# Layer 0 of a two-layer transformer kernel: the first projection K-tile by K-tile behind its modulation, and a step's transposes ahead of its values

## The chip, the core and the metric

The kernel runs on one core of a Trainium2 chip. A core has TensorE (PE in the profile; its weight loads are PEld), VectorE (DVE), ScalarE (ACT), GpSimd (POOL), and SyncE (SP), whose queue starts nearly all DMA transfers here. The metric is device time in microseconds, the median of several runs; the profile is one execution of the same program.

## The reference, cut to what matters

512 latent tokens of width 1024, and 256 context tokens, pass two layers. Layer 0 has sixteen heads of 64, in four groups: each of four key/value heads serves four query heads. Two groups attend in a window (with a sink), two to all tokens. Everything is float32.

```python
mx = (silu(c) @ mod_w[l] + mod_b[l])            # six parts of 1024: shift, scale, gate, twice
hx = _rms(x, norm_mix_w[l]) * (1.0 + scx1) + shx1     # modulated input; the same for ctx with c_ctx
q, k, v = heads(hx @ w_in)                      # q and k: RMS norm per head, rotary for latent tokens
p = softmax(q @ k.T * scale)                    # window mask and sink in the first two groups
out = (p @ v) @ w_out
x = x + gx1 * out
x = x + gx2 * swiglu(_rms(x, norm_ffn_w[l]) * (1.0 + scx2) + shx2)
```

Layer 1 is a differential attention with the same frame. The change does not touch it.

## The kernel before, in words

Tokens lie in six tiles of 128: 0 to 3 latent, 4 and 5 context; `CTX_FIRST` is the order 4, 5, 0, 1, 2, 3. Products that need full precision are made of three fast ones: an operand is split into a high part (`hi`, rounded by ACT) and a remainder (`lo`, a subtraction), and hi x hi, hi x lo and lo x hi are summed in PSUM. The 1024 inputs are eight K-tiles; a projection of one token tile for one key/value head (384 columns: four queries, key, value) is 24 matmuls.

The kernel is written as one program in a natural order, and a scheduler then sets the order of each engine's instructions by dependencies, buffers and priorities. Each engine keeps its order at run time.

**The start.** `start_mod(n)` makes shift and scale (parts 0 and 1) for quarter n of the width, two K-tiles: mod weights (0.5 MB pieces) come by DMA, matmuls with a 32-wide padded operand give partial rows (`mod`, L171), ACT copies them (`modr`, L174), two small matmuls with a selection matrix add them up as columns (`modcol`, L179), and DVE adds the bias (`modc`, `aff`). In between, each token tile is normed (`nh`, L843 and L844), turned by TensorE (`npt`, L848) and copied to `xT` (L849). Then all of `xT` is modulated K-tile by K-tile (L854) and split into `hT`, or `hTc` for context (L859, L860). Only behind all this are the weights of the first head loaded and split (`weights0`; `wir`, `wih`, `wil`, L309 and L310), and `in_proj0` projects tile after tile (`inps`, L405 to L407), each summed over all eight K-tiles at once.

**A tile of a projection** is copied by ACT (`qkv`), normed per head and rotated (`rotate`: DVE, ACT, and POOL for `rs_q`, `qy`, `kd` and the copy of the values, `vv`), and turned by TensorE (`qpt`, `kpt`) into `qt` and `kT`.

**The attention of layer 0**, `attend0`, is a generator for one step, that is one key/value head and one tile of queries. It makes scores of two query heads (`sc`, L509), maxima on DVE, exponentials on ACT (`Pt`, L523), and scales them on POOL (L533), twice with a `yield` behind each. Then for each pair of key blocks of 128 it turns the probabilities (`ppt`, L543; two PSUM banks, tr0 and tr1), copies them out (`PT`, ACT and DVE by turns, L548 and L546), and sums values (`av`, L553; two halves of the output side by side in the array). Probabilities lie in tiles of one head, six buffers. `Staggered` emits the first scores of a step, then the last step's whole rest, then the second scores. Meanwhile the next head is projected, a tile per step; its `qkv` has two buffers. In the fourth head's loop the output projection (`ops`) starts.

## Time and profile before

| what | us |
|---|---|
| runs, lowest, median, highest | 1823.11, 1824.57, 1825.61 |
| the profiled execution: its own time, its span | 1825.45, 1823.7 |
| TensorE busy in the span | 1752.0 |
| VectorE, ScalarE, GpSimd busy | 1002.0, 825.5, 641.8 |
| start to the first scores of layer 0 | 72.4 |
| layer 0's mixer from there to the first FFN matmul | 72.4 to 447.6 |
| FFN of layer 0 | 447.6 to about 1040 |
| layer 1's mixer, then its FFN | to about 1453, then to the end |

In the lines shown below, a group of instructions has line, engine, operation, tiles written and read, shapes and count; then busy time and the mean in ns of one; then idle time of the engine ahead of them, and what ended it. A row of the timeline has start, duration, engine, line, operation, tiles and count, and in brackets an idle time. A row of waits reads: who waited for whom, us in total, times, longest. A duration on TensorE includes the pipeline; the time from start to start tells what an instruction really takes up.

### The profile page before, as it was taken

To read this page: it belongs to the slowest core of one execution; us is meant where nothing else is said; L and a number is where in the kernel's file an instruction comes from. 1 tells how busy PE (TensorE), PEld (TensorE's weight loads), DVE (VectorE), ACT (ScalarE), POOL (GpSimd) and SP (SyncE) were. 2 spreads that over 40 slices of the span, in tenths; PEclk is the share of its full clock that TensorE was granted. 3 is DMA by queue.
4 is the path that set the end of the run, shared out by engine and by line. 5 is a ranking of instruction groups with operands and counts; after the bars stand their busy time and mean duration, and the time that the engine had idled before them with its cause. 6 is when DMAs were issued, how large, how long until landed. Compare 5 with 4: busy or idle time off the path is not lost. (4 is left out here: it accounts for less than half of the span.)

```text
span 1823.7 us, 26198 instructions
## 1 busy us (share of the span) xinstructions
PE 1752.0 (96%) x9958; PEld 1458.2 (80%) x9958; DVE 1002.0 (55%) x1703; ACT 825.5 (45%) x1726; POOL 641.8 (35%) x840
## 2 busy tenths in 40 slices
PE   6999999999999999999999899999998999999998
PEld 4877676667888888888888789999986888888886
DVE  4664545443355555545552657777675455655652
ACT  6555555544354444333331656666664532222220
POOL 2764554632053443222220466666643200000000
PEclk8999999999999999999999899999999999999999
DMA  9111322302543334334330311111103233232221
GB/s 314 46 44 55 96 73 99 131 13 76 180 149 117 103 104 140 115 127 126 117 105 3 102 35 59 44 45 44 42 25 104 90 97 102 82 104 93 93 93 47
DMA packets 152478, 165.65 MB, mean 91 GB/s; under 512 B 16480, under 2 KB 139936, under 8 KB 152352
## 3 DMA queue, kind: packets, MB, share of 16 engines
q1 hardware_dynamic: 152000, 163.77, 28.1%
q8 instruction: 78, 1.28, 0.3%
q14 instruction: 48, 0.39, 0.1%
q10 hardware_dynamic: 352, 0.21, 0.0%
HBM read 159.73 MB, written 4.22 MB: 90 GB/s over the span
## 5 line engine op out<-in xcount | busy, mean ns | idle before, releaser
L750 PE MATMUL pg<-hT,wgh 128*128 128x512 f32 (+1 forms) x736 | 244.8, 386 | 2.2 <-ACT hT L293 2.2
L750 PE MATMUL pu<-hT,wuh 128*128 128x512 f32 (+1 forms) x736 | 244.1, 385 | 0.0
L412 DVE TENSOR_TENSOR dps<-dps,g 128x512 f32<-128x512 f32 x200 | 135.7, 697 | 131.3 <-PE dps L801 126.7
L799 PE MATMUL dps<-wdh,hdh 128*128 128x512 f32 x440 | 176.2, 401 | 5.3 <-DVE x L413 3.5
L800 PE MATMUL dps<-wdl,hdh 128*128 128x512 f32 x440 | 174.0, 396 | 0.0
L801 PE MATMUL dps<-wdh,hdl 128*128 128x512 f32 x440 | 166.4, 396 | 0.0
L750 PEld LDWEIGHTS pg<-hT,wgh 128*128 128x128 f32 x736 | 137.2, 189 | 32.7 <-ACT hT L293 2.4
L750 PEld LDWEIGHTS pu<-hT,wuh 128*128 128x128 f32 x736 | 137.1, 189 | 28.5
L750 PE MATMUL pg<-hT,wgl 128*128 128x512 f32 (+1 forms) x368 | 141.9, 386 | 0.0
L750 PE MATMUL pu<-hT,wul 128*128 128x512 f32 (+1 forms) x368 | 141.5, 384 | 0.0
L413 DVE TENSOR_TENSOR x<-x,dps 128x512 f32<-128x512 f32 x200 | 133.3, 683 | 3.3
L405 PE MATMUL inps<-wih,hT 128*128 128x384 f32 x384 | 133.1, 347 | 0.4 <-ACT qkv L451 0.2
L406 PE MATMUL inps<-wil,hT 128*128 128x384 f32 x384 | 130.6, 340 | 0.0
L407 PE MATMUL inps<-wih,hT 128*128 128x384 f32 x384 | 130.6, 340 | 0.0
L198 ACT ACTIVATE modw<-modw,cols 128x256 f32<-128x256 f32 x192 | 81.9, 498 | 69.4 <-DMA modw<-in_mod_w_dram 66.4
L799 PEld LDWEIGHTS dps<-wdh,hdh 128*128 128x128 f32 x440 | 82.7, 188 | 27.6 <-DVE x L413 4.4
L310 DVE TENSOR_TENSOR wul<-wur,wuh 128x1024 fp32r<-128x1024 f32 x44 | 54.6, 1241 | 89.3 <-ACT wuh L309 89.3
L801 PEld LDWEIGHTS dps<-wdh,hdl 128*128 128x128 f32 x440 | 82.6, 188 | 20.2 <-issue 0.4
L750 PE MATMUL pg<-hTc,wgh 128*128 128x256 f32 x352 | 98.3, 283 | 0.5 <-ACT hTc L293 0.2
L750 PE MATMUL pu<-hTc,wuh 128*128 128x256 f32 x352 | 98.2, 282 | 0.0
L800 PEld LDWEIGHTS dps<-wdl,hdh 128*128 128x128 f32 x440 | 82.8, 188 | 17.6
L777 DVE TENSOR_TENSOR pu<-sg,pu 128x768 f32<-128x768 f32 (+1 forms) x44 | 36.5, 829 | 108.3 <-PE pu L750 94.4
(235 smaller groups left out, 4306.3 us busy)
## 6 DMA issues: line engine op xcount, KB each, us to landing
modw<-in_mod_w_dram SPq DMA_DIRECT2D x96, 512.0 KB, 4.0
wgr<-in_ffn_w_in_dram SPq DMA_DIRECT2D x44, 512.0 KB, 3.4
wur<-in_ffn_w_in_dram SPq DMA_DIRECT2D x44, 512.0 KB, 3.4
wdr<-in_ffn_w_out_dram SPq DMA_DIRECT2D x44, 512.0 KB, 3.5
wir<-in_od_w_in_dram SPq DMA_DIRECT2D x96, 128.0 KB, 2.3
x<-in_x_dram SPq DMA_DIRECT2D x8, 512.0 KB, 3.9
wir<-in_ev_w_in_dram SPq DMA_DIRECT2D x16, 256.0 KB, 2.7
wor<-in_ev_w_out_dram SPq DMA_DIRECT2D x8, 512.0 KB, 4.4
```

The source lines that it names most:

```text
L198: nc.scalar.activation(pr[:, k], w[:, k], AF.Copy, scale=cols[:, kk:kk + 1])
L310: (sub or nc.vector).tensor_sub(lo, raw, f32(hi))
L405: nc.tensor.matmul(ps, hs[0][:, k, :], a, start=k == 0, stop=False)
L406: nc.tensor.matmul(ps, hs[0][:, k, :], b, start=False, stop=False)
L407: nc.tensor.matmul(ps, hs[1][:, k, :], a, start=False, stop=k == KT - 1)
L412: nc.vector.tensor_mul(tmp, ps, g[:, n * 512:(n + 1) * 512])
L413: eng.tensor_add(xt[:, n * 512:(n + 1) * 512], xt[:, n * 512:(n + 1) * 512], tmp)
L750: nc.tensor.matmul(ps[:, s0:s1], a, cols_T(b, s0, s1)[:, k, :], start=k == 0 and q == 0, stop=k == KT - 1 and q == 2)
L777: nc.vector.tensor_mul(pu, sg, pu)
L799: nc.tensor.matmul(ps, hh, a, start=j == 0, stop=False)
L800: nc.tensor.matmul(ps, hh, b, start=False, stop=False)
L801: nc.tensor.matmul(ps, hl, a, start=False, stop=j == nj - 1)
```

## The change

- **First head, start.** The modulation of parts 0 and 1 is made a quarter at a time (`start_mods`), both parts in one PSUM tile and one `modr`. Behind each quarter `start_h` modulates and splits its two K-tiles (some of the modulation goes from DVE to ACT), and `project` sums only these K-tiles, for six token tiles that stand in six PSUM banks. The head's weights come unit by unit (`unit0`) right behind the mod weights of their quarter, through `raw_tile` with two buffers, and their remainders go from DVE to POOL. Half of the `xT` copies go from ACT to DVE.
- **Modulation columns**, in all chunks: two transposes and a DVE reduce over four partial rows (`mod_cols`) instead of two matmuls with the selection matrix.
- **Attention of layer 0.** Four heads' probabilities lie in one tile `P4`, two buffers. All transposes of a step come first, the turned blocks are written back into `P4`, then a new `yield`, then all values. `Pairs` emits first scores of a step, the last step's transposes, second scores, the last step's values. In the fourth head's loop the output projection of a tile follows half a step later.
- `qkv` has five buffers instead of two, for all heads of layer 0.

```diff
-PBUF0 = 6
+QBUF = 5
@@ mod_chunk
-        pc2 = p_1.tile([P, nb, 2], F32, name="modcol", tag=bank)
+        add_mod(l, part, k0, k1, mod_cols(r, p_1.tile([P, nb, P], F32, name="modcol", tag=bank)), 2)
+
+    def mod_cols(r, ps):
+
+        nb = ps.shape[1]
         for b in range(nb):
-            nc.tensor.matmul(pc2[:, b, :], r[:, b * P:(b + 1) * P], sel2, start=True, stop=True)
-        add_mod(l, part, k0, k1, pc2, 2)
+            nc.tensor.transpose(ps[:, b, :], r[:, b * P:(b + 1) * P], ident)
+        m = small.tile([P, nb, 2], F32, name="mcol", tag=f"mcol{nb}")
+        nc.vector.tensor_reduce(m, ps.rearrange("p b (j r) -> p b r j", r=32)[:, :, 0:2, :], AX.X, ALU.add)
+        return m
@@
-    def project(ps, t, ws, c0, c1):
+    def project(ps, t, ws, c0, c1, ks=range(KT)):
...
-        for k in range(KT):
+        for k in ks:
@@ in_proj0
-            ps = acc_tile("inps", 384, one=0) if b else p_sc.tile([P, 1024], F32, name="inps", tag="sc")[:, :384]
-            project(ps, t, ws, 0, 384)
-            raw = wp.tile([P, 384], F32, name="qkv", tag="qkv", bufs=2)
+            if banks:
+                ps = banks[t]
+            else:
+                ps = acc_tile("inps", 384, one=0)
+                project(ps, t, ws, 0, 384)
+            raw = rp.tile([P, 384], F32, name="qkv", tag="qkv", bufs=QBUF)
@@ attend0
-        Pt = [None] * 4
+        P4 = mp.tile([P, 4, TOK], F32, name="Pt", tag="Pt", bufs=2)
+        Pt = [P4[:, h, :] for h in range(4)]
...
-        for g0 in range(0, nk, 2):
-            PTs = []
-            for kc in range(g0, min(g0 + 2, nk)):
...
-                PT = mp.tile([P, 4, P], F32, name="PT", tag="PT", bufs=4)
-                if kc % 2:
-                    nc.vector.tensor_copy(PT, pt)
-                else:
-                    nc.scalar.copy(PT, pt)
-                PTs.append((kc, PT))
-
-            for kc, PT in PTs:
...
+        for kc in range(nk):
+            pt = tr_tile("ppt", [P, 4, P], one=kc % 2)
+            cs = slice(kc * P, (kc + 1) * P)
+            for h in range(4):
+                nc.tensor.transpose(pt[:, h, :], Pt[h][:, cs], ident)
+
+            if kc % 2:
+                nc.vector.tensor_copy(P4[:, :, cs], pt)
+            else:
+                nc.scalar.copy(P4[:, :, cs], pt)
+        yield
+
+        for kc in range(nk):
+            for j in range(2):
+                nc.tensor.matmul(av[64 * j:64 * j + 64, :], vv[:, vt[kc], :], P4[:, j::2, kc * P:(kc + 1) * P],
+                                 start=kc == 0, stop=kc == nk - 1)
@@
+    class Pairs:
...
+        def push(self, gen):
+
+            self.flush()
+            self.new, self.last = gen, self.new
             next(gen)
+            if self.last:
+                next(self.last)
+
+        def step(self):
+
+            next(self.new)
             self.flush()
@@
+    def start_mods(n):
+
+        ps = tr_tile("mod", [P, 2, 256])
         for part in range(2):
...
+        r = start.pool.tile([P, 512], F32, name="modr", tag="modr", bufs=1)
+        nc.scalar.copy(r, ps.rearrange("p a n -> p (a n)"))
+        m = mod_cols(r, tr_tile("modcol", [P, 4, P]))
+        for part in range(2):
+            add_mod(0, part, 2 * n, 2 * n + 2, m[:, 2 * part:2 * part + 2], 2)
+
+    def start_h(n, segs):
+
+        ks = slice(2 * n, 2 * n + 2)
+        for s0, s1 in segs:
+            i = s0 // SEQ
+            for k in range(2 * n, 2 * n + 2):
+                z = xT[:, k, s0:s1]
+                sc, sh = aff[0][:, 0, k, i:i + 1], modc[0][:, 0, k, i:i + 1]
+                if k % 2:
+                    nc.scalar.activation(z, z, AF.Identity, bias=sh, scale=sc)
+                else:
+                    nc.vector.tensor_scalar(z, z, sc, sh, ALU.mult, ALU.add)
+            hi, lo = (cols_T(j, s0, s1)[:, ks, :] for j in range(2))
+            nc.scalar.copy(hi, xT[:, ks, s0:s1])
+            (nc.gpsimd if i else nc.vector).tensor_sub(lo, xT[:, ks, s0:s1], f32(hi))
@@
-    start_mod(0)
-    start_mod(1)
+    start_mods(0)
+    ws = [unit0(0, 0, wp.pool, nc.gpsimd)]
...
+    banks = {t: acc_tile("inps", 384) for t in CTX_FIRST[:2]}
+    for t in (0, 2):
+        two = p_sc.tile([P, 2, 512], F32, name="inps", tag="sc")
+        banks.update({t + a: two[:, a, :384] for a in range(2)})
+    for n in range(4):
+        if n:
+            start_mods(n)
+            ws.append(unit0(0, n, wp.pool, nc.gpsimd))
+        start_h(n, ((SEQ, TOK), (0, SEQ)) if n else ((SEQ, TOK), (0, SEQ // 2), (SEQ // 2, SEQ)))
+        for t in CTX_FIRST:
+            project(banks[t], t, ws, 0, 384, range(2 * n, 2 * n + 2))
...
-    att = Staggered()
+    att = Pairs()
...
-                if b == 3 and hp == 0 and 0 < t <= 5:
+                if b == 3 and hp == 1 and 0 < t <= 5:
```

83 lines of the change are left out of this document (39 added, 44 removed).

## The prediction

> **What bounds the kernel now.** I read the page's first two parts, then a table of stretches, then TensorE's timeline where its clock or its busy share falls, then waits and groups of the layer-0 mixer. Of the page: the span, TensorE's busy time, its busy share and its granted clock in 40 slices of 45.6 us.
>
> ```profile
> span 1823.7 us, 26198 instructions
> PE   6999999999999999999999899999998999999998
> PEclk8999999999999999999999899999999999999999
> ```
>
> TensorE is busy nearly throughout, so what counts is PE time that does no work. Slice 1 is the only bad one, and the first part of the change sits there. The table of stretches (busy time of each engine, then granted clock, DMA share, GB/s):
>
> ```profile
> 0.00:6.70 6.70, 0.00 (x0) 0.00 (x0) 0.00 (x0) 3.40 (x6) 0.54 (x6) 1.00 0.69 235
> 6.70:20.00 13.30, 11.50 (x74) 6.11 (x74) 3.08 (x8) 7.22 (x14) 2.68 (x6) 1.00 1.07 397
> 20.00:28.00 8.00, 5.29 (x50) 4.06 (x51) 4.38 (x9) 6.67 (x15) 3.66 (x7) 1.00 1.07 374
> 28.00:40.80 12.80, 9.81 (x85) 5.53 (x83) 8.98 (x20) 6.95 (x13) 1.86 (x1) 0.67 1.04 330
> 40.80:46.00 5.20, 5.20 (x19) 5.20 (x20) 5.20 (x11) 3.63 (x7) 3.75 (x1) 0.51 0.27 79
> 46.00:72.40 26.40, 26.01 (x155) 25.14 (x156) 18.76 (x38) 12.38 (x29) 19.21 (x25) 1.00 0.09 21
> 72.40:92.30 19.90, 17.86 (x98) 16.12 (x97) 11.55 (x37) 12.32 (x35) 17.74 (x30) 0.91 0.27 75
> 92.30:310.00 217.70, 212.53 (x1503) 157.32 (x1501) 116.03 (x310) 121.36 (x324) 112.45 (x175) 0.99 0.23 71
> 350.00:447.60 97.60, 91.49 (x461) 67.28 (x461) 38.54 (x71) 41.16 (x84) 30.69 (x33) 1.00 0.10 33
> ```
>
> Until 40.8 the DMA engines are full and TensorE has small work only; from 40.8 to 72.4 the first head's projection runs with the DMA idle. That is the serial pair which the change folds together. The attention (92 to 447) looks full, but a busy PE need not be efficient; the timeline shows where (start, duration, count, and idle time in brackets):
>
> ```profile
> 374.45 1.08 PE L553 MATMUL av<-PT,vv 128*64 128x256 f32 x8
> 375.47 1.09 PE L543 MATMUL ppt<-cst,Pt 128*128 128x128 f32 x8
> 376.80 0.65 PE L553 MATMUL av<-PT,vv 128*64 128x256 f32 x4 [0.24 <-ACT PT L548]
> 377.38 0.66 PE L543 MATMUL ppt<-cst,Pt 128*128 128x128 f32 x4
> 377.97 0.65 PE L553 MATMUL av<-PT,vv 128*64 128x256 f32 x4
> 378.55 0.66 PE L543 MATMUL ppt<-cst,Pt 128*128 128x128 f32 x4
> ```
>
> By starts, one key block of values and one of transposes, alternating, take 378.55 - 377.38 = 1.17 us. Two blocks of each in one alternation take 376.56 - 374.45 = 2.11 us (without the 0.24 of waiting) where two alternations take 2.34. Each alternation costs 0.23 us.
>
> **Part 1: the start.** All K-tiles came after all modulations; now each quarter (two K-tiles, 36 matmuls over six tiles) follows its own modulation. Before and now, the end of the start on TensorE (mod: modulation matmuls; modcol: their turn to columns; inps: projection):
>
> ```order
> L171 MATMUL mod<-modw,s_pad 32x256 x12
> L179 MATMUL modcol<-cst,modr 128x2 x2
> L171 MATMUL mod<-modw,s_pad 32x256 x8
> L179 MATMUL modcol<-cst,modr 128x2 x2
> L405 MATMUL inps<-wih,hTc_112 128x384
> ```
>
> Now, behind the third quarter's projection:
>
> ```order
> L411 MATMUL inps<-wil,hT_110 128x384
> L412 MATMUL inps<-wih,hT_111 128x384
> L868 MATMUL mod<-modw,s_pad 32x256 x2
> L182 MATMUL modcol<-cst,modr 128x128 x4
> L410 MATMUL inps<-wih,hTc_112 128x384
> ```
>
> Only one quarter is left behind the last modcol, but nothing stands between the two on TensorE to cover the modulation's way through ACT and DVE. On ACT, the second quarter's modr copy now stands behind the norms of all six tiles (nh, xT); it was two copies, the first of them ahead of the fifth and sixth tile. Before:
>
> ```order
> L849 COPY xT<-npt 128x4x128
> L843 ACTIVATE nh,nss<-x_201 128x1024
> L174 COPY modr<-mod 128x256
> L849 COPY xT<-npt 128x4x128 x2
> L843 ACTIVATE nh,nss<-x_203 128x1024
> ```
>
> Now the sixth tile's copies come first:
>
> ```order
> L889 CAST hT_110<-xT 128x2x256
> L907 COPY xT<-npt 128x4x128 x2
> L314 CAST wih<-wir 128x768
> L885 ACTIVATE xT<-xT,modc_106,aff_108 128x256
> L889 CAST hT_110<-xT 128x2x256
> L871 COPY modr<-mod 128x512
> ```
>
> The second quarter's modulation moved behind that row.
>
> The rows that price this (timeline and groups):
>
> ```profile
> 28.01 1.07 ACT L849 COPY xT<-npt 128x512 f32<-128x512 f32 x2
> 44.45 0.52 PE L407 MATMUL inps<-wih,hTc 128*128 128x384 f32 x1
> 44.77 0.52 PE L405 MATMUL inps<-wih,hTc 128*128 128x384 f32 x1
> 46.13 0.34 PE L406 MATMUL inps<-wil,hTc 128*128 128x384 f32 x1
> 46.30 0.34 PE L407 MATMUL inps<-wih,hTc 128*128 128x384 f32 x1
> 72.43 0.39 PE L509 MATMUL sc<-kT,qt 128*128 128x256 f32 x2
> 92.35 0.60 PE L543 MATMUL ppt<-cst,Pt 128*128 128x128 f32 x4
> L849 ACT COPY xT<-npt 128x512 f32<-128x512 f32 x12 | 6.6, 590 | 4.8 <-PE npt L848 4.7
> L309 ACT CAST wih<-wir 128x768 fp32r<-128x768 f32 x5 | 4.1, 832 | 0.0
> L860 DVE TENSOR_TENSOR hT<-xT,hT 128x512 fp32r<-128x512 f32 x6 | 5.0, 849 | 0.0
> ```
>
> A projection matmul is issued every 0.17 us (46.13 to 46.30) at full clock, every 0.32 at a granted 0.5 (44.45 to 44.77).
>
> - SP's queue: up to the last mod weight go 13.5 MB (six tiles and 16 pieces of 0.52 MB, four weight units of 0.39, 0.4 of constants). The stretches moved 1.6, 5.3 and 3.0 MB by 28 us; the other 3.6 MB at 374 GB/s land by 38 us. Four weight units now go between; the four tiles of x have four pieces and one unit ahead of them instead of six pieces, and come earlier.
> - Second quarter: the six norms end at 29.1 (28.01 + 1.07), so modulation, cast and first matmul come at about 32. From there 36 x 0.174 = 6.3 us a quarter: 38.5, then 45, and with 1 us of small waits 46. By then the last weights have long landed.
> - Last quarter: modr copy 0.6 (512 wide, as xT), four transposes 0.5, DVE's reduce and adds 0.9 (part 2), modulation 0.6 to 1.0 (256 and 512 wide), a wih cast (0.83) that stands between on ACT, hi cast 0.6: about 5 us in which TensorE stands. Then 6.3 us, 0.6 of waiting for DVE's lo part, and 1.7 because the clock falls after such a gap (0.91 over 19.9 us in the stretch at 72.4 is 1.8 lost): end at about 60.5.
> - Then: before, the first softmax transposes (ppt) stand at 92.35, with 213 inps, 16 sc, 24 qpt and 11 kpt issued; now with 285, 8, 24 and 12, since the second head's projection fills TensorE while six tiles are rotated. From 60.5: 141 x 0.174 = 24.5, 36 transposes of q and k at the 0.12 of a ppt 4.3, scores 1, and about 3.5 of waiting for the first rotated tile on POOL. That is 93.8. Before, 72 more projections (12.5) less eight scores (0.9) would be done at 103.9. **Gain 10.1.**
>
> POOL takes the first head's weight remainders from DVE, and the second head's stand ahead of the rotations there:
>
> ```profile
> L149 POOL TENSOR_TENSOR rs_q<-rs_q,neghalf 128x5 f32<-128x5 f32 x24 | 28.5, 1188 | 1.2
> L310 POOL TENSOR_TENSOR wil<-wir,wih 128x768 fp32r<-128x768 f32 x11 | 20.1, 1829 | 3.7 <-ACT wih L309 3.6
> L454 POOL TENSOR_TENSOR qy<-qy,rs_q 128x320 f32<-128x320 f32 x24 | 17.3, 722 | 0.9
> L461 POOL TENSOR_TENSOR kd<-qy,kd 128x128 fp32r<-128x128 f32 x24 | 11.7, 488 | 10.6 <-ACT kd L460 5.1 <-ACT es L527 2.1 <-PE sc L509 1.6
> ```
>
> By the order, up to the first kd POOL does three rs_q (3.6), one wil, one qy and small copies: 10 us from 60.5, against 8.4 us of projections on TensorE. Hence the wait, 2.5 with 1 for the clock. Later tiles have 4 us of projection each ahead of them, and 3 us of POOL.
>
> Ends for this part: without any wait after 38 + 5 + 6.3 the projection ends at 49, 11 us more gain; with the last three quarters (108 matmuls) at half clock, 108 x 0.146 = 15.8 us worse, a loss of 5.7.
>
> A rule of the Trainium skill speaks against this part: "TensorE: Matmul & The Clock Gate", section "HAM oscillation — how this bites in real kernels", tells that bursts per K-tile with a DMA wait between leave the clock halved in each, and to do all K-tiles of a tile before the next wait. By that rule the gain is the lower end. The clock of 0.67 from 28 to 40.8 agrees with it, but there TensorE had gaps and small matmuls; here three quarters follow each other without a gap by my walk. I take the upper half.
>
> **Part 2: modulation columns.** Four small matmuls (two calls) become two transposes and a DVE reduce.
>
> ```profile
> 154.28 0.57 PE L179 MATMUL modcol<-cst,modr 128*128 128x2 f32 x4
> 154.71 0.37 PE L509 MATMUL sc<-kT,qt 128*128 128x256 f32 x1
> L227 DVE TENSOR_TENSOR modc<-modcol,bcol 128x4 f32<-128x4 f32 x12 | 1.9, 157 | 6.4 <-PE modcol L179 6.3
> ```
>
> 0.43 us become 2 x 0.11 (by ppt rows): 0.2 saved in each of 16 chunks outside the start, **3.2 us**. The reduce isn't in the trace; between modc (0.16) and a mean-square reduce of 320 (0.48) it is hidden, as DVE is about half busy. The lower end is no gain where TensorE waits anyway.
>
> **Part 3: attention.** Key block by key block of one step on TensorE (third head; ppt: transposes of probabilities, av: values, sc: scores):
>
> ```order
> L553 MATMUL av<-PT,vv 64x256 x2
> L543 MATMUL ppt<-cst,Pt 128x128 x4
> L553 MATMUL av<-PT,vv 64x256 x2
> L543 MATMUL ppt<-cst,Pt 128x128 x4
> L171 MATMUL mod<-modw,s_pad 32x256 x8
> ```
>
> Now four blocks of transposes, with scores and a modulation between, come ahead of two blocks of values:
>
> ```order
> L548 MATMUL ppt<-cst,Pt 128x128 x8
> L516 MATMUL sc<-kT,qt 128x256 x2
> L516 MATMUL sc<-kT,qt 128x512 x2
> L516 MATMUL sc<-kT,qt 128x256 x2
> L516 MATMUL sc<-kT,qt 128x512 x2
> L548 MATMUL ppt<-cst,Pt 128x128 x4
> L170 MATMUL mod<-modw,s_pad 32x256 x8
> L548 MATMUL ppt<-cst,Pt 128x128 x4
> L558 MATMUL av<-Pt,vv 64x256 x4
> ```
>
> Over the whole layer the order has 91 runs of av before and 64 now, ppt 102 and 100: 27 fewer switches at 0.23 are **6.2 us**. Ends: 0, and twice that. Waits of TensorE in the attention, and the copies concerned:
>
> ```profile
> PE av L553 <- ACT PT L548: 2.6, 5, 0.7
> PE av L553 <- DVE PT L546: 1.0, 1, 1.0
> L548 ACT COPY PT<-ppt 128x512 f32<-128x512 f32 x52 | 30.6, 588 | 54.1 <-PE ppt L543 54.0
> L546 DVE COPY PT<-ppt 128x512 f32<-128x512 f32 x48 | 33.0, 687 | 31.6 <-PE ppt L543 31.6
> L523 ACT ACTIVATE Pt<-sc,nm 128x768 f32<-128x768 f32 x32 | 28.8, 902 | 10.4 <-DVE nm L522 5.3 <-POOL wol L310 4.1 <-PE ppt L543 0.9
> ```
>
> Values no longer wait for a copy just started: 3.6 us go, but the transposes, two banks for all blocks, now wait for the copies; I keep **1.8**. The copies are as many and as large, written back into P4. With projections run ahead, 108 of 200 av calls precede the last projection instead of 120: one step more without filler, **1 us** back.
>
> Sum: 10.1 + 3.2 + 6.2 + 1.8 - 1 = 20.3. The profiled execution took 1825.45, 0.9 above the median of three (1824.57): 1825.45 - 20.3 = 1805.
>
> **Rivals.**
>
> - Cold quarters (the rule above): the gain shrinks by 15.8 to 4.5, 1821. For it: the clock at 28 to 46. Against it: 36 dense matmuls a quarter.
> - Attention no better: values and transposes stay interleaved enough that part 3 gives nothing: 1825.45 - 12.3 = 1813. For it: ppt runs hardly change.
> - Slower: transposes lose their cover. A bank's cycle is 0.44 of transposes, 0.16 of pipeline, 0.64 of copy, so 0.62 a block against 0.44; with an exp (0.90) ahead of each second copy 0.63 us a block is lost. Of 100 blocks 52 lie beyond the first two of a step: 33 us, 1838. It decides above 24/52 = 0.46 a block. Against it: scores and projections stand between, by the order.
> - Better: the start loses nothing after the last weights: 1794.
>
> **Numbers.** Likeliest 0.55 (1798 to 1812), attention no better 0.17, cold quarters 0.11, slower 0.07, better 0.10. 0.2% is 3.6 us, about what a measurement tells from no change. Cold quarters lie at its edge, half on each side: faster 0.87, within 0.06, slower 0.07. The range 1795 to 1820 leaves out the slower case, most of the cold one and the better one's far end.
>
> **What would show it.** Right: the first ppt at about 94 with 285 projections done, the clock back at 1.0 by 35, av runs near 64, waits of av on PT gone. Wrong: inps 0.32 apart between 32 and 46; ppt waiting for PT or Pt copies by tens of us; a gap before the last quarter far from 5 us.

## The result, and the profile after

The changed kernel took 1837.99 us in the median of four runs (1836.03 to 1838.75), the kernel before 1823.84 beside it (1822.75 to 1825.61): ratio 1.0077, 95% interval 1.0065 to 1.0089. It is 14 us slower, where 20 us of gain were forecast. The page of the changed kernel, whose profiled execution was its slowest run (1838.75): span, TensorE's busy time, its busy share and its granted clock in 40 slices of 45.9 us.

```profile
span 1837.0 us, 26108 instructions
PE 1739.0 (95%) x9910; PEld 1452.8 (79%) x9910; DVE 1002.2 (55%) x1715; ACT 824.6 (45%) x1722; POOL 644.6 (35%) x844
PE   7899999789999999999999899999998999999998
PEclk9999999899999999999999999999999999999999
```

TensorE is busy 13 us less than before (1752.0) in a span 13 us longer, and the slice at 321 to 367 us, where the busy share and the clock read 9 and 9 before, reads 7 and 8. The stretches that answer to those of before:

```profile
28.00:40.80 12.80, 11.88 (x118) 8.78 (x120) 5.61 (x14) 7.60 (x13) 5.04 (x4) 1.00 0.70 220
40.80:46.00 5.20, 5.20 (x39) 4.13 (x39) 2.57 (x8) 3.50 (x5) 2.73 (x2) 1.00 0.89 293
60.00:72.40 12.40, 10.58 (x46) 10.22 (x47) 3.16 (x7) 5.33 (x11) 6.13 (x7) 0.75 0.17 48
350.00:366.00 16.00, 10.66 (x29) 7.44 (x29) 1.39 (x2) 0.00 (x0) 5.37 (x4) 0.59 0.32 98
350.00:447.60 97.60, 83.17 (x399) 61.25 (x400) 29.01 (x56) 32.40 (x68) 27.62 (x28) 0.92 0.12 38
```

The start now has TensorE at work from 28 us on, but between 60 and 72.4 it stands for part of the time and runs at a lower clock. And in a place that the prediction did not look at, 350 to 366 us, where the fourth head's attention and the output projection run, TensorE issued 29 matmuls in 16 us. From 350 to 447.6 it issued 399 where the kernel before issued 461.

How far the kernel was ahead or behind can be followed by the same work: the time at which TensorE has issued as much. Against the profile of before it was 7 us ahead at 50, level at 72, 5 to 7 ahead from 310 to 340, 6 behind at 360, and 12 behind at the first FFN matmul (459.2 against 447.6). So there are two losses, one of the start's own and one near 355, and a gain of the attention between them.

**Near 355.** TensorE, changed kernel (rows with a wait, and two of the projection that follows them):

```profile
346.41 0.50 PE L721 MATMUL ops<-woh,hT 128*128 128x512 f32 x1 [0.45 <-ACT woh L314]
351.35 0.80 PE L722 MATMUL ops<-wol,hT 128*128 128x512 f32 x1 [2.66 <-POOL wol L315]
355.42 0.79 PE L722 MATMUL ops<-wol,hT 128*128 128x512 f32 x1 [2.42 <-POOL wol L315]
358.21 0.80 PE L721 MATMUL ops<-woh,hT 128*128 128x512 f32 x1 [1.57 <-DVE x L418]
359.23 0.63 PE L723 MATMUL ops<-woh,hT 128*128 128x512 f32 x1
359.66 0.63 PE L721 MATMUL ops<-woh,hT 128*128 128x512 f32 x1
```

The output projection (`ops`) waits for the remainders of its weights (`wol`, made on POOL from `woh`, which ACT makes), and then runs 0.43 us a matmul (359.23 to 359.66) instead of 0.23, since the granted clock was 0.5 from 349.5 to 363.1. ACT made the first of these weights late: the changed kernel's ACT, and POOL's last remainder; then the matching three rows of the kernel before.

```profile
317.86 0.37 ACT L560 COPY o<-av 128x256 f32<-128x256 f32 x1 [1.07 <-PE av L558]
318.13 2.00 ACT L314 CAST woh<-wor 128x1024 fp32r<-128x1024 f32 x2
353.02 2.35 POOL L315 TENSOR_TENSOR wol<-wor,woh 128x1024 fp32r<-128x1024 f32 x1
```

```profile
312.86 0.38 ACT L475 CAST kT<-kpt 128x256 fp32r<-128x256 f32 x1
313.13 2.01 ACT L309 CAST woh<-wor 128x1024 fp32r<-128x1024 f32 x2
345.39 2.37 POOL L310 TENSOR_TENSOR wol<-wor,woh 128x1024 fp32r<-128x1024 f32 x1
```

Before, the first cast stood behind the last key transposes of the fourth head. Now it stands behind the copy of the third head's last values, though the first weights had been asked for at 295.1 and 296.5. A late first cast puts off all eight: the raw weights have two buffers, so the third transfer is issued at 322.12, when POOL's first remainder is done (322.1), and so on down the line.

**The start.** TensorE, changed kernel: the second quarter's modulation and first matmul, the third quarter's last matmul, the last modulation, the last quarter's beginning and end, the first ppt.

```profile
31.89 1.93 PE L868 MATMUL mod<-modw,s_pad 128*32 128x256 f32 x32
35.95 0.60 PE L182 MATMUL modcol<-cst,modr 128*128 128x128 f32 x4
39.31 0.44 PE L410 MATMUL inps<-wih,hTc 128*128 128x384 f32 x1 [0.86 <-ACT hTc L889]
55.30 0.34 PE L412 MATMUL inps<-wih,hT 128*128 128x384 f32 x1
55.57 0.63 PE L868 MATMUL mod<-modw,s_pad 128*32 128x256 f32 x4
56.98 0.65 PE L182 MATMUL modcol<-cst,modr 128*128 128x128 f32 x4 [0.79 <-ACT modr L871]
61.25 0.69 PE L410 MATMUL inps<-wih,hTc 128*128 128x384 f32 x1 [3.62 <-ACT hTc L889]
69.68 0.34 PE L412 MATMUL inps<-wih,hT 128*128 128x384 f32 x1
103.43 0.38 PE L548 MATMUL ppt<-cst,Pt 128*128 128x128 f32 x2
```

The first head's projection ended at 69.7, one us ahead of before, and the first ppt came at 103.4 with 285 projection matmuls issued, half a us better than the break-even of 103.9. ACT shows what it did while the last quarter's modulation was due:

```profile
49.01 0.83 ACT L314 CAST wih<-wir 128x768 fp32r<-128x768 f32 x1 [3.15 <-DMA wir<-in_ev_w_in_dram]
52.97 0.84 ACT L314 CAST wih<-wir 128x768 fp32r<-128x768 f32 x1 [3.12 <-DMA wir<-in_ev_w_in_dram]
55.61 0.83 ACT L314 CAST wih<-wir 128x768 fp32r<-128x768 f32 x1 [1.81 <-DMA wir<-in_ev_w_in_dram]
56.35 0.58 ACT L871 COPY modr<-mod 128x512 f32<-128x512 f32 x1
```

Three casts of the second head's weights stood ahead of the last quarter's `modr` on ACT, and each waited for a transfer. They held `modr` by 0.2 us at most, though: the last four modulation matmuls end at 56.2, because on TensorE they stand behind the third quarter's projection (55.30, then 55.57). Their weights were there by then: the last transfer was issued at 37.6, and none took over 7.6 us.

**The attention.** In the changed trace values run in 64 groups (91 before), and the waits of TensorE from 92 to 447 have no row of av for a copy of probabilities any more:

```profile
PE sc L516 <- ACT Pt L530: 5.8, 10, 0.9
PE ops L722 <- POOL wol L315: 5.1, 2, 2.7
PE ops L721 <- DVE x L418: 3.1, 2, 1.6
```

### The profile page after: what moved, and what is told of

Read it like the earlier page. It is cut to its first block, busy times and chain, and to the rows that moved or that the text cites. A ratio compares the mean times of both kernels' runs of the same rounds, so it can differ in the third digit from the quotient of the medians.

```text
span 1837.0 us, 26108 instructions
## 1 busy us (share of the span) xinstructions
PE 1739.0 (95%) x9910; PEld 1452.8 (79%) x9910; DVE 1002.2 (55%) x1715; ACT 824.6 (45%) x1722; POOL 644.6 (35%) x844
## 5 line engine op out<-in xcount | busy, mean ns | idle before, releaser
L315 POOL TENSOR_TENSOR wil<-wir,wih 128x768 fp32r<-128x768 f32 x46 | 86.5, 1885 | 28.4 <-ACT wih L314 28.1
```

The lines of the kernel that those rows point to most:

```text
L315: (sub or nc.vector).tensor_sub(lo, raw, f32(hi))
```

## The experiments

Each kernel is the one before or the changed one with the edit shown. "First FFN" is the start of the first FFN matmul in the profiled execution, the end of layer 0's mixer; it is the surest number of a trace here, because the runs of one kernel spread by up to 12 us (before: 1820 to 1828 in one set). Two profiles of the kernel before differ by 2.0 us in it. "First ppt" has the number of projection matmuls issued until then in brackets. Each set was measured beside runs of before of its own, with medians from 1823.8 to 1824.6.

| kernel | median us | ratio to before, 95% | first ppt | first FFN |
|---|---|---|---|---|
| before, first profile | 1824 | | 92.3 (213) | 447.6 |
| before, second profile | 1820.4 (one run) | | 91.3 (213) | 445.6 |
| changed | 1838.0 | 1.0065 to 1.0089 | 103.4 (285) | 459.2 |
| start alone | 1848.4 | 1.0114 to 1.0148 | 98.8 (216) | 470.3 |
| start alone, three PT buffers | 1833.2 | 1.0034 to 1.0068 | 99.6 (216) | 453.4 |
| attention alone | 1823.1 | 0.9978 to 1.0005 | 92.0 (215) | 437.7 |
| columns alone | 1828.0 | 1.0010 to 1.0028 | 93.7 (213) | 446.8 |
| attention and columns | 1819.2 | 0.9954 to 0.9979 | 95.0 (215) | 439.1 |
| changed, two qkv buffers | 1828.0 | 1.0005 to 1.0031 | 100.2 (216) | 446.5 |
| changed, three qkv buffers | 1840.6 | 1.0071 to 1.0113 | 100.7 (237) | 457.8 |
| changed, wol on DVE | 1828.3 | 1.0003 to 1.0028 | 103.0 (285) | 447.7 |
| two buffers: modulations with priority | 1851.0 | 1.0135 to 1.0165 | 97.8 (213) | 445.8 |
| two buffers: POOL relieved | 1827.1 | 1.0008 to 1.0030 | 97.3 (213) | 444.3 |
| two buffers: whole tiles | 1826.7 | 0.9997 to 1.0016 | 100.3 (237) | 446.5 |
| two buffers: halves | 1825.4 | 0.9998 to 1.0017 | 98.7 (213) | 448.0 |
| two buffers: ACT's queue freed | 1822.8 | 0.9967 to 0.9991 | 96.3 (216) | 442.9 |
| the same, POOL relieved | 1823.4 | 0.9984 to 1.0007 | 97.0 (215) | 444.7 |
| whole tiles, ACT's queue freed | 1827.5 | 1.0008 to 1.0031 | 101.8 (216) | 447.1 |
| attention and columns, two banks | 1820.7 | 0.9967 to 0.9994 | 94.6 (215) | 438.5 |

### The parts apart, and the late weights

**Start alone**: the new start in the kernel before; attention, columns of the other chunks and two qkv buffers as before, qkv in the pool of the change.

```diff
 # against the changed kernel
-QBUF = 5
+QBUF = 2
+PBUF0 = 6
-    att = Pairs()
+    att = Staggered()          # attend0, its tiles and the place of ops: as before
```

> The kernel before with the first part of the change alone: the quarters of the first head, with their columns by two transposes and a reduce. Attention, qkv buffers and the columns of all other modulations are those of before. Three theories. Fourth head (mine now): the change's loss sits where the output projection starts, between 344 and 366 us, because the remainders of its weights (wol) come late on POOL for projections that were put together in a bunch; the start itself gains nothing, since its last quarter stands behind a gap of 4 us and runs half a quarter at half clock. Then this kernel has its first ppt within 2 us of 92.3 corrected for the projections run ahead, and takes 1824, plus or minus 4. Cover (rival on record): the start is a gain and the attention's transposes lose their cover; this kernel takes 1813 to 1816. Fillers (rival): projections run ahead through five qkv buffers are missing later; with two buffers here nothing is missing: 1824.

Measured 1848.4: all three theories missed. It was 6.5 us late at the first ppt and 22.7 at the first FFN matmul; 13.7 of that came between the first and the 48th ops (344.7 to 377.8, before 337.8 to 357.2), with a wait of 4.62 us for wol. So the stall near 355 does not come from the attention's new order, and the start alone is a loss.

**Attention alone**: P4, `Pairs` and the later output projection in the kernel before.

```diff
 # against the kernel before: attend0, Pairs and
-                if b == 3 and hp == 0 and 0 < t <= 5:
+                if b == 3 and hp == 1 and 0 < t <= 5:
```

> The kernel before with the attention part alone (P4, all transposes of a step ahead of its values, output projection half a step later); start, modulation columns and two qkv buffers as before. Fourth head: by the order six of the eight wol remainders stand ahead of the second tile's operand on POOL, as in the kernel before, so the stall at 344 to 366 is 4 us at most, while the fewer changes between ppt and av give 5: about 1822 to 1824. Cover: 1836 or more, with waits of ppt on the copies through heads one to three. Fillers: 1819, since nothing runs ahead.

1823.1, first FFN matmul at 437.7, 10 us ahead of the first profile of before. The place where the changed kernel stalls is quiet (345.5 for the 48th ops), and of ppt for the copies there are 1.8 us of waiting in heads one to three. "Cover" is refuted. That the median shows less than the trace is taken up below.

**Two qkv buffers** in the changed kernel:

```diff
-QBUF = 5
+QBUF = 2
```

> The changed kernel with two qkv buffers instead of five, nothing else. By the order its fourth head is then that of the attention part alone, with the wol remainders earlier on POOL. Fourth head: the stall of 344 to 366 mostly goes, 1828, plus or minus 3. Cover: no difference, 1838. Fillers: 1826 to 1828 as well, but then the gain comes evenly wherever projections were missing, and not between 344 and 366 alone.

1828.0 and first FFN matmul at 446.5: the stall is gone (48th ops at 354.4 instead of 365.9), and "Cover" falls again. ACT's first casts of that kernel, to be held against those at 318.13 above:

```profile
307.19 0.59 ACT L476 CAST qt<-qpt 128x512 fp32r<-128x512 f32 x1 [0.17 <-PE qpt L474]
307.67 1.06 ACT L314 CAST woh<-wor 128x1024 fp32r<-128x1024 f32 x1
```

**Remainders on DVE** in the changed kernel:

```diff
-            oproj = OutProj(0, out_units(wp.pool, ev_w_out), o_t, xs, opa.pool)
+            oproj = OutProj(0, out_units(wp.pool, ev_w_out, (nc.vector,)), o_t, xs, opa.pool)
```

> The changed kernel with the remainders of layer 0's output weights made on DVE instead of POOL, nothing else. DVE is idle for 7.5 and 8.2 us between 348 and 366. Fourth head: the two waits for wol (2.7 and 2.4 us) go, with most of the half clock behind them; 8 to 12 us back, 1826 to 1830, first FFN matmul at 449 instead of 459. Cover and Fillers: no difference, 1838.

1828.3, first FFN matmul at 447.7. Taking the work from POOL takes the loss away too: 11.5 us by that mark. What is lost is thus that the remainders are late. Why they are late, the two buffers tell more of: with them the casts came 10 us earlier.

### Why the weights come late

The tiles' places in SBUF, as the program assigns them, give a reason. The output weights' pool lies at the right end of a partition, and its first tile begins at byte 163808. The pool of the first and third head, on the left, ends at 162112 before. The change moves qkv into it: with two buffers it ends at 163520, with five at 168128, over the first output-weight tile. In the start alone, whose attention pool is 1.9 KB larger, it ended at 165376 with two buffers. In each kernel where the two overlap the order has the first cast behind the third head's last values, and in none of the others.

**Three qkv buffers** (the pool ends at 165056) in the changed kernel, and **three PT buffers** (it ends at 163328) in the start alone:

```diff
-QBUF = 5
+QBUF = 3
```

> The changed kernel with three qkv buffers instead of five. By the layout of SBUF the first tile of layer 0's output weights (woh) begins at byte 163808 of a partition; with two buffers the third head's pool, to which the change has moved qkv, ends at 163520, with three at 165056. Overlap (mine now): the output weights can't be split until the third head is finished with that pool, so that its two first casts stand behind the third head's last values, the remainders come late on POOL and the fourth head stalls: as long as with five buffers, first FFN matmul at 458 plus or minus 2, 1836 to 1840. Fillers (rival): projections that run ahead are the cause; three buffers are nearer to two than to five: 1828 to 1832, with no wait for wol between 340 and 370.

```diff
-                PT = mp.tile([P, 4, P], F32, name="PT", tag="PT", bufs=4)
+                PT = mp.tile([P, 4, P], F32, name="PT", tag="PT", bufs=3)
```

> The kernel with the first part of the change alone, as run before, with three PT buffers instead of four: the pool ends 2 KB lower, at 163328, and no longer overlaps the output weights (with four it ended at 165376). Overlap: the 13.7 us that that kernel lost between the first and the 48th ops go, and what is left is the start's own loss of 7 to 9: 1831 to 1834, first FFN matmul at 455 to 457. If the overlap has nothing to do with it: 1848 again.

1840.6 with the first FFN matmul at 457.8, and 1833.2 with 453.4. One buffer of 1.5 KB more brings the stall back in full, 2 KB less in another tile takes it away, 15 us of the median. "Fillers" is refuted: three buffers are as bad as five. It is shown that the overlap makes the loss; whether the casts wait for the qkv tiles alone or for all of that pool, was not tried apart. By the layout only qkv tiles reach into the output weights, and they are last read at 289.2 in the changed kernel, 29 us ahead of the first cast; the third head's last values, behind which that cast stands, read `vv` of the same pool. That speaks for the whole pool.

### What the start loses

With two buffers the changed kernel differs from "attention and columns" (below) by the start alone: 446.5 against 439.1 at the first FFN matmul. That is 7.4 us of loss for the start, to be explained.

**Modulations with priority**, in the changed kernel with two buffers:

```diff
-            start_mods(n)
+            with tc.high_priority(300):
+                start_mods(n)
```

> The changed kernel with two qkv buffers, and the modulations of quarters two to four emitted with a higher priority, so that by the order the last quarter's stand ahead of most of the third quarter's projection on TensorE and ahead of the second head's weight casts on ACT. Gap (mine): the 3.6 us gap ahead of the last quarter and the half clock behind it (some 15 matmuls by 0.15) go: end of the first head's projection at 63 instead of 69, first ppt at 94 to 95 instead of 100.2, 1822. Rival: POOL, which has to rotate six tiles after the projection's end, is bound by other things than that end: first ppt within 2 us of 100, 1828.

The projection's end stayed at 69.2 and the first FFN matmul came at 445.8: a miss. TensorE made the last modulation by 50.9, but then ACT waited for a cast of the second head:

```profile
58.15 0.83 ACT L314 CAST wih<-wir 128x768 fp32r<-128x768 f32 x1 [4.70 <-DMA wir<-in_ev_w_in_dram]
58.89 1.30 ACT L885 ACTIVATE xT<-xT,modc,aff 128x256 f32<-128x256 f32 x2
```

```profile
56.64 0.87 DVE L887 TENSOR_SCALAR xT<-xT,aff,modc 128x256 f32<-128x256 f32 x2
```

DVE began its share of the last quarter's modulation at 56.64, ACT 2.3 us later. The total, 1851.0, has most likely another cause: the scheduler's order differs in layer 1 too, whose mixer took 417 us in the trace instead of 389.

**POOL relieved** (two buffers):

```diff
-            nc.gpsimd.tensor_copy(vv[:, t, :], raw[:, 320:384])
+            (nc.vector if banks else nc.gpsimd).tensor_copy(vv[:, t, :], raw[:, 320:384])
-            nc.gpsimd.tensor_sub(kd[:, 1], kb, f32(kd[:, 0]))
+            (nc.vector if banks else nc.gpsimd).tensor_sub(kd[:, 1], kb, f32(kd[:, 0]))
-            ws = [unit0(b + 1, u, wp.pool, nc.gpsimd) for u in range(4)]
+            ws = [unit0(b + 1, u, wp.pool, nc.gpsimd if b else nc.vector) for u in range(4)]
```

> The changed kernel with two qkv buffers, and the first head's value copies and key remainders, and the second head's weight remainders, made on DVE instead of POOL. POOL (mine): between the end of the first projection and the first ppt POOL is the bound, busy 41 of 44 us; six copies (0.24 to 0.5), four to six key remainders (0.46 to 0.7) and one or two weight remainders (1.85) less give 5 to 7 us: first ppt at 94 to 95 instead of 100.2, 1822. Rival: a chain through ACT, DVE and POOL for each tile is the bound, and POOL's share only looks full: 1 to 2 us.

First ppt at 97.3, 2.4 us better with three matmuls fewer counted in, first FFN matmul 2.2 better: between the two, nearer the rival.

**Whole tiles** and **halves** (two buffers). The first takes all four quarters' `start_mods` and `start_h`, and then

```diff
+    for t in CTX_FIRST:
+        project(banks[t], t, ws, 0, 384)
```

> The changed kernel with two qkv buffers, and the first projection tile by tile over all eight K-tiles, behind the four quarters' modulations, which still come quarter by quarter; the scheduler may begin a tile's early K-tiles before the last modulation. Pipelining (mine): the changed start loses because the six tiles' sums all come to their end within a few us, at 66 to 70, so that their copies, norms and rotations, beside which the projection ran before, now stand behind it, and POOL takes some 3.3 us a tile. With whole tiles the first is copied out some 5 us earlier than the last: first key remainder at 70 to 73 instead of 78.5, first scores at 78 instead of 84, first ppt at 95 to 97 with as many projections, 1823 to 1826. End of the projection (rival): only its end counts, 69 to 71 here too: first ppt at 99 to 101, 1828.

and the second projects K-tiles 0 to 3 of all tiles behind the second quarter, 4 to 7 behind the last.

> The changed kernel with two qkv buffers, and the first projection in two halves of four K-tiles each instead of four quarters. Pipelining: between the changed start and whole tiles: a tile's last half takes 2.1 us instead of 1.0, the first key remainder comes at 72 to 75, first ppt at 96 to 98, 1824 to 1827. End of the projection: 99 to 101 and 1828, unless that end itself moves.

Pipelining is right in its first steps and not in its sum. With whole tiles the first key remainder came at 64.0 instead of 78.5, the first scores at 74.8 instead of 84.0, and the first ppt at 100.3 with 21 more projections done (3.7 us), as good as 96.7. But at the first FFN matmul nothing was left (446.5). On TensorE from 70 to 150 there were new waits of scores for probabilities, 6.4 us in four places, and a granted clock of 0.5 from 133.3 to 140.1. Halves had the first key remainder at 69.4, the first ppt at 98.7, and 448.0 at the first FFN matmul.

**ACT's queue freed** (two buffers): modulation and `start_h` of a quarter are emitted ahead of the projection of the quarter before, and the high parts of the second head's first two weight units are made on POOL.

```diff
+    start_h(0, ((SEQ, TOK), (0, SEQ // 2), (SEQ // 2, SEQ)))
     for n in range(4):
-        if n:
-            start_mods(n)
-            ws.append(unit0(0, n, wp.pool, nc.gpsimd))
-        start_h(n, ...)
+        if n < 3:
+            start_mods(n + 1)
+            ws.append(unit0(0, n + 1, wp.pool, nc.gpsimd))
+            start_h(n + 1, ...)
...
+            ... unit0(b + 1, u, wp.pool, nc.gpsimd, nc.gpsimd.tensor_copy if b == 0 and u < 2 else None)
```

> The changed kernel with two qkv buffers; each quarter's modulation is emitted ahead of the quarter before's projection, and the high parts of the second head's first two weight units go from ACT to POOL. By the order nothing of the second head stands on ACT ahead of the last quarter's modulation, where the changed kernel waited 3.1, 3.1 and 1.8 us for such weights to land. ACT queue (mine): the last quarter's projection begins at 55 to 57 instead of 61, the first head's projection ends at 62 to 65 instead of 69, first ppt at 94 to 96 (216 projections) instead of 100.2, 1822 to 1824. Rival: POOL, which gets two more casts and must rotate six tiles, takes it back: first ppt 99 to 101, 1828.

The projection ended at 65.3 instead of 69.0, the first ppt came at 96.3 with 216, the first FFN matmul at 442.9: 3.6 of the 7.4 us are found. The last quarter of this kernel, TensorE and ACT:

```profile
48.62 0.64 PE L868 MATMUL mod<-modw,s_pad 128*32 128x256 f32 x8
57.30 0.52 PE L410 MATMUL inps<-wih,hTc 128*128 128x384 f32 x1 [1.83 <-ACT hTc L889]
```

```profile
49.33 0.59 ACT L871 COPY modr<-mod 128x512 f32<-128x512 f32 x1 [4.23 <-PE mod L868]
56.64 0.60 ACT L889 CAST hTc<-xT 128x512 fp32r<-128x512 f32 x1
```

ACT waits for the modulation instead of a transfer, `modr` is copied 7 us earlier than in the changed kernel, and TensorE waits 1.83 us instead of 3.62 (3.33 with two buffers). The 7 us are those by which the modulation comes earlier on TensorE (48.62 instead of 55.57). The freed queue shows in the next step: ACT modulates as soon as DVE has the factors, which it did not in the run with priority, and no cast stands between that and `hTc`, where one of 0.8 us stood in the changed kernel. The two edits were not run apart here; that run, with the modulations alone moved, left the projection's end where it was (69.2).

**The other 3.8 us**: the same with POOL relieved (of value copies and key remainders), and whole tiles with the second head's high parts on POOL.

> The kernel just run for ACT's queue (modulations a quarter ahead, the high parts of the second head's first two weight units on POOL; it took 1822.8), and the first head's value copies and key remainders on DVE instead of POOL. If, once ACT's queue is free, POOL's rotation of six tiles is what remains of the start's loss (3.8 us at the first FFN matmul against the same kernel with the start of before): first ppt at 93 to 94 instead of 96.3, first FFN matmul at 440 instead of 442.9, 1819 to 1821. If a chain of small steps for each tile remains, not POOL's time: no difference, 1822 to 1824.

> The changed kernel with two qkv buffers, the first projection in whole tiles behind the quarters' modulations, and the high parts of the second head's first two weight units on POOL. The first key remainder comes at 64 as with whole tiles before. If the start's loss is ACT's queue and the six tiles' common end together, both are gone here: first ppt at 92 to 95, first FFN matmul at 439 to 441, 1818 to 1821. If waits of scores for probabilities between 115 and 140 take the place of what is saved, as with whole tiles alone: first FFN matmul at 445 to 447, 1825 to 1827.

444.7 and 447.1 at the first FFN matmul: neither moved it the right way. With POOL relieved the first ppt came 30.0 us after the projection's end instead of 31.0, and that end came 1.7 later (67.0), so POOL's time is at most a small part of the rest. With whole tiles the second outcome came, nearly as expected: scores waited 6.0 us in five places for probabilities between 70 and 150, where they waited 1.6 in two with ACT's queue freed. These waits took what was saved, so whether the tiles' common end is part of the rest stays open. The stretches from 72 to 88 and to 104 show where the two kernels part, of ACT's queue freed, then of attention and columns with the start of before:

```profile
72.00:88.00 16.00, 10.43 (x44) 9.06 (x45) 10.71 (x34) 11.44 (x32) 14.47 (x24) 0.58 0.09 25
88.00:104.00 16.00, 16.00 (x112) 15.20 (x112) 10.95 (x35) 9.53 (x32) 12.21 (x23) 0.99 0.02 5
```

```profile
72.00:88.00 16.00, 14.11 (x83) 11.98 (x83) 13.22 (x35) 13.18 (x36) 14.43 (x22) 1.00 0.24 67
88.00:104.00 16.00, 15.49 (x104) 14.47 (x104) 10.53 (x28) 8.69 (x28) 12.95 (x22) 1.00 0.11 30
```

While the first tiles are rotated TensorE has little to do, and then a stretch of 10 to 14 us at half clock begins at 74 to 80. All eleven kernels with the new start and two or three qkv buffers have one, and no kernel with the start of before has more than 3.4 us there. That this half clock is the rest of the loss fits in size (half of 10 busy us, an estimate from the first row), but no run took it away by itself: it is argued, not shown. The two kernels with the new start and five buffers have no half clock there either, with some 70 projections more ahead of their first ppt; with the remainders on DVE that kernel comes to 447.7, not below the 446.5 of two buffers. It differs in more than this stretch, so it does not decide the matter.

### The columns, the sum, and a better kernel

**Columns alone**, in the kernel before (`mod_cols` instead of the two matmuls with the selection matrix):

> The kernel before with the modulation columns alone: two transposes and a reduce on DVE, in every chunk, start included. The prediction's second term: 3.2 us saved in 16 chunks outside the start, so 1820.6. Rival: where TensorE waits for the copy of the sums anyway, the saved 0.2 us of each chunk is only a longer wait: no difference, 1823 to 1825.

1828.0, ratio 1.0010 to 1.0028: no gain, rather a small loss. The saving itself is there. In the 16 chunks outside the start, `modcol` took TensorE 6.9 us from its first start to the next instruction's before, and 3.8 now; a pair of rows of this kernel:

```profile
155.37 0.40 PE L182 MATMUL modcol<-cst,modr 128*128 128x128 f32 x2
155.53 0.72 PE L514 MATMUL sc<-kT,qt 128*128 128x256 f32 x4
```

At the first FFN matmul (446.8) it can't be told from the two profiles of before. The three us were not on the path there; why the runs are slower is open (layer 1's mixer took 390.5 us in this trace, 3 to 6 more than in the two of before).

**Attention and columns**, with the start of before and two buffers:

> Attention and modulation columns of the change, with the start of before and two qkv buffers (no overlap with the output weights). If the two parts add up: the attention part alone was 1823.1 in the median, less what the columns give: 1820 to 1823; first FFN matmul at 436 plus or minus 2 (437.7 with the attention alone, 447.6 before). If the columns give nothing: 1823.

1819.2 in the median of five runs, ratio 0.9954 to 0.9979: the only version whose whole interval lies more than 0.2% below the kernel before, and the one to keep. It beats both kernels. In the medians it is 3.9 us faster than the attention alone, so the columns are a loss by themselves (1828.0) and look like a gain on top of the attention (the two intervals just touch); this is not explained.

**The kernel before once more**, unchanged:

> The kernel before, unchanged, for a second profiled execution. The attention part alone was 9.9 us ahead of the first profile of before at the first FFN matmul, but only 0.8 in the medians of the runs. If executions differ in layer 0 by what surrounds them, this one reaches the first FFN matmul some us earlier than 447.6; if the attention's gain is real there and given back in layer 1, 447 plus or minus 1, and layer 1's mixer (first lps to its FFN) takes 387 plus or minus 1.

The answer lies between. The first FFN matmul came at 445.6, two us ahead of the first profile, and layer 1's mixer took 384.6 instead of 387.6 (from the first `lps`, at 1049.4 in the first profile, to the first matmul of its FFN, at 1437.0; the 1453 in the table of before is too late for that), so two executions differ by 2 us in layer 0 and by 5 in all. Against the two, the attention's gain at the end of layer 0 is 8 to 10 us, beyond that spread. But layer 1's mixer took 386.5 to 393.0 in all the other kernels except the one with priority (417) and the start alone with three PT buffers (395.8, profiled in its slowest run): above both of before except in three (386.5, 386.8 and 387.5). Its code is the same, its order is not (TensorE's order differs in over twenty places between before and changed). A loss of about 3 us there fits the medians; it was not taken apart.

**Two banks** for the output projection's sums in the fourth head's loop, in that version:

```diff
-                    oproj.sums(t - 1, 0)
+                    oproj.sums(t - 1)
```

> Attention and modulation columns of the change with the start of before and two qkv buffers (1819.2), and the output projection's sums in the fourth head's loop in both accumulator banks by turns instead of one. TensorE waited there 4.7 us in four places for DVE to empty the one bank. If those waits go: 1815 to 1817, first FFN matmul at 435. If the values (av), which use the second bank, wait instead: 1819 to 1822.

1820.7, first FFN matmul 438.5 instead of 439.1: no difference, as the second expectation had it.

## Why the prediction was wrong, point by point

By the first FFN matmul the parts add up from kernel to kernel. From the mean of the two profiles of before, 446.6: attention -8.9 (437.7), columns +1.4 (439.1), new start +7.4 (446.5), five buffers +12.7 (459.2). That is 12.6 of the 14 us. Each is one profile, and two of one kernel differ by 2.0, so the columns' +1.4 is not more than that. By the medians of the runs the same steps are -0.8, -3.9, +8.8 and +10.0: the two large terms hold by both measures, the two small ones don't agree.

- **Not in the sum at all: qkv's five buffers, 12.7 us.** The prediction took them only as what lets projections run ahead, and costed that at 1 us. It did not ask where the buffers lie. They were moved to another pool and made five, and the pool grew over the first tile of the output weights. Of a buffer that is moved or multiplied, what comes to lie on it later is part of the change. This step was missing; everything else together would have been 4 us slower than before (1828.0), still no gain.
- **Part 1, second quarter "at about 32": measured 39.31.** This is the step of the walk that failed first; the later ones held in length. I set 2.9 us from the end of the norms to the first matmul. The norms ended 2 to 3 us later (the sixth tile's npt at 31.36 on TensorE, behind the first quarter's projection), the 32 modulation matmuls only then, `modr` at 33.9, `modcol` at 35.95 behind twelve projections on TensorE's queue, and from there 3.4 us to the first matmul. The quarter ends came at 47.5, 55.3 and 69.7, where 38.5, 46 and 60.5 stood: 9 us late each, 7.3 of it from that quarter's beginning and the rest from within it, where a `modcol` and sixteen modulation matmuls stand among the projections. The gap ahead of the last quarter, forecast as 5, was 5.7 from the last modulation to the first matmul, by the steps listed: one cast of 0.8 stood between, and ACT's modulation took 1.3 where I had 0.6 to 1.0. From there to the projection's end it took 8.4, where 8.6 stood. (The prediction's own parts add up to 59.6 for that end, not to 60.5.)
- **Part 1, the rest.** From the projection's end to the first ppt I had 33.3 us, and it took 33.7. (POOL's first kd came 10.2 us after that end, where 10 stood; the rows named there make up only 6.1 of it.) But I counted 72 projections run ahead as 12.5 us of gain. By the same work the changed kernel was some 3 us ahead of before at 104 and 3 to 5 behind at 120. Between the two TensorE was busy 13.1 of 16 us, where it was 15.9 before, and from 110.6 to 117.4 the clock was 0.5. That the projections were missing there is how I read it. Without them, with two buffers, the start is a loss of 7.4 at the first FFN matmul, where a gain of 10.1 was forecast. The break-even by work done was a fair sum and a wrong measure, since it prices cover that is used up early as if it were gained.
- **Part 2: right at its place, not shown at the end.** 3.0 us saved on TensorE (forecast 3.2). In the runs the columns were 3.4 us slower alone and 3.9 faster on top of the attention, and at the first FFN matmul nothing of them shows.
- **Part 3: right at the end of layer 0, not in the runs.** 6.2 + 1.8 - 1 = 7.0 was forecast, 8.9 measured at the first FFN matmul with this part alone, but 0.8 in the medians (ratio 0.9978 to 1.0005), which can't be told from no change. Changes between groups cost about 7 us less from the first ppt to the first ops. (Each TensorE instruction's time to the next start, less the median between two of its own group, less the waits, summed where the group changes: 28.7 and 28.0 in the two profiles of before, 21.3 with the attention alone; cut into groups in other ways, the difference is up to 9.) The waits were as long as before (6.5 against 7.0 and 7.4), so the 1.8 was not there. By the same work the attention was about 13 us ahead of the first profile at 340, and gave 3 to 4 back by 447, where the output projection, half a step later, waits for its one bank (4.7 us in the version with the columns); a second bank did not win them back.
- **The rivals.** The slower one had 1838, the time measured, and is nevertheless wrong: transposes did not lose their cover (waits of ppt for Pt on ACT or DVE, 0.7 us in the changed kernel, 2.6 with the attention alone). The price of one mechanism happened to be that of another: luck. "Attention no better" falls by the 8.9 at the first FFN matmul, "better" by the gap of 5.7. Cold quarters: quarters two and three ran 0.17 us apart at a clock of 1.00, as I had argued, but the last one did stand behind a gap and ran at half clock until 66.2, which cost some 2.5 us by estimate (half of 61.25 to 66.2), where 1.7 stood. By the rule of the Trainium skill quoted there ("TensorE: Matmul & The Clock Gate", section "HAM oscillation — how this bites in real kernels") a DMA wait of some 3 to 5 us ahead of a K-tile's burst leaves that burst at half clock; the trace agrees for the quarter behind a wait of 3.62 us (here for ACT), and the one behind a wait of 0.86 us ran at 1.00.
- **The signs.** Three that were named for a right prediction came true (64 groups of av, no waits of av for copies, the clock at 1.0 by 35) in a kernel 14 us slower; the first ppt, at 103.4 instead of 94, did not.

## What to carry to other kernels

Look up where a buffer lies before and after an edit that moves it or adds to it, and what later tile comes to lie over it: here 1.5 KB decided over 12 us, 250 us later in the program. Walk a pipelined start through every queue that it shares with other work: here the last modulation stood behind a quarter's projection on TensorE, and, once moved ahead there, behind a cast on ACT that waited 4.7 us for its transfer. And price work that runs ahead only by what TensorE does after it is used up.

## What the runs showed of the hardware

The granted clock falls to 0.5 in stretches that are multiples of 3.4 us (3.4, 6.8, 10.2, 13.7), and not at the same places in two executions of one program. The first profile of before had half clock from 32.3 to 46.0, the second only from 26.4 to 29.8; this is the stretch from 28 to 40.8 in the second:

```profile
28.00:40.80 12.80, 9.64 (x103) 6.28 (x95) 9.14 (x20) 7.96 (x16) 1.87 (x1) 0.93 1.02 321
```

The prediction had read the 0.67 there as a trait of the kernel. Both executions ended the first projection at 70.6 plus or minus 0.1, so in this place no cost of the clock is left at that end. The Trainium skill ("TensorE: Matmul & The Clock Gate", section "What's actually happening") states a free-running window of 3413 ns; the lengths seen agree.
